# Attention stage of a decoder trunk: items joined over heads and groups, another order of branches, more work in the background

## The chip, the cores and the metric

The kernel runs on one core of a Trainium2 chip. The metric is the time of one execution on the device in microseconds (us). A core has five engines that run their own instruction streams and wait for one another through semaphores: TensorE (PE, with the weight loads PEld listed apart), VectorE (DVE), ScalarE (ACT), GpSimd (POOL) and SyncE (SP). Matrix products land in PSUM, in banks of 128 x 512 float32; everything else lies in SBUF. Transfers go over queues; in this kernel SP's queue carries the weights and ACT's a few others.

## The reference

A trunk of two layers on x of 512 tokens x 1024 channels. Layer 0 is a short convolution mixer and a squared-ReLU MLP. Then one shared key and value projection is made, layer 1 is sparse attention on it and a second MLP, and a final norm ends it. What matters here is the attention:

```python
kv = (h @ w_kv).reshape(B, S, 6, N_KV_GROUPS, HEAD_DIM)      # 6 parts of 4 groups x 64
k_cmp = compress_blocks(kv[:, :, 0], cmp_pe_k, phi_k_w1, phi_k_w2)   # 31 blocks of 32 tokens, stride 16
v_cmp = compress_blocks(kv[:, :, 1], cmp_pe_v, phi_v_w1, phi_v_w2)   # silu(flat @ w1) @ w2
k_sel, v_sel, k_win, v_win = kv[:, :, 2], kv[:, :, 3], kv[:, :, 4], kv[:, :, 5]
qg = h @ w_qg                          # 16 heads x 64, and 3 gates per head
q, gates = qg[..., :1024] / 8, sigmoid(qg[..., 1024:])
# for each block of 128 queries, each of 4 groups, each of 4 heads in the group:
o_c = softmax(q @ k_cmp.T + bias) @ v_cmp       # compressed branch
o_s = softmax(q @ ks.T + bias) @ vs             # selected blocks
o_w = softmax(q @ kw.T + bias) @ vw             # sliding window
o = gate0 * o_c + gate1 * o_s + gate2 * o_w
x = x + o @ w_o
```

With 512 tokens the selection (16 blocks of 64) and the window (512) hold all earlier tokens, so the second and third branch are both full causal attention, each with its own keys and values. The bias depends on the distance of the tokens and the head.

## The kernel before

**Arithmetic.** Every float32 operand is split into a high and a low float16 part, and a product is three matmuls into one accumulator (`mm3`, lines 339 to 341): high x high, low x high, high x low. Splits are made by ACT (high part) and DVE or POOL (low part).

**Weights.** They are cut into pieces of up to 512 KB in one list, `pieces`, in order of use. SP's queue loads them into `wst`; `convert_piece` makes `whi` on ACT (line 193) and `wlo` on DVE (line 194). `next_piece` hands out the next one, and `ahead_fine` converts up to two pieces ahead in steps between the matmuls.

**The stage that changes** lies between the last matmul of the first MLP and the first of the second. Each step of a projection is a generator that issues a few matmuls and yields:

- `keys(br)`, `values(br)`: keys and values of the second (br 0) and third (br 1) branch, into `KD` and `VT`; `gates()`; `queries(g)`: the four heads of group g into `Q`, whose low parts POOL makes (line 739).
- `raw(which)`: the raw keys or values of the compressed branch. 48 matmuls of 512 columns into two banks; then for each of the two banks DVE scales it into `at_s` (line 757), ACT and DVE split it into `kr_hl` (lines 360, 362), and six transfers on SP's queue (lines 763 to 765) lay it out in `big`. `kr_hl` has one buffer.
- `phi(which)`: the compressing MLP, 96 matmuls of 155 columns that read `big`, a Silu on ACT (line 793), a split, and a second small product.
- `out_proj(g)`: output projection of groups g and g + 1.

`load_T(g)` loads the bias rows of a group (issued on ACT's queue, line 621) and copies every sixteenth column to `Tc` on DVE (line 625).

A lead-in runs `keys(0)`, `keys(1)`, `values(0)`, `values(1)`, `gates` and `queries(0)` to their ends. Then come 144 **items**. A `Full` item is one head, one block `qb` of 128 queries and one branch: `nk` = 128 (qb + 1) keys. It goes through five steps:

- st0: scores on PE (lines 914, 915, bank b), bias and minimum on DVE (line 919), exponential with sum on ACT (line 922);
- st1: float32 transposes on PE (line 928, bank c), high part `at_ph` on ACT (line 931);
- st2: low part `at_pl` on DVE (line 934);
- st3: the product with the values on PE (lines 946 to 948, bank d); after the last head, gates and sums on DVE and POOL;
- st4: after a block's last part, its transposition into `ot`, which `out_proj` reads.

A `Cmp` item is the same for the compressed branch, for four heads of one group at once.

**Order.** The loop over items issues st0 of item i, then some background, then the later steps of earlier items (`lead`: 2, 3, 4 and 6 items back). A scheduler makes each engine's final order from the issued program; every engine then runs its own list in that order. The background is a chain of generators, resumed by a credit per item:

```python
items = full(0) + full(1) + cmps(0) + cmps(1) + full(2) + cmps(2) + cmps(3) + full(3)
# background: raw(0), q1, phi(0), raw(1), phi(1), q2, q3, then out_proj(0)
credit += 1.7 if i < 64 else 0.9          # yields per item
```

An item that needs something not yet made (its queries, the compressed keys and values) drains the background until it is there.

Of the kernel before, what the change touches and what calls it, by code (L numbers as in the profile page):

```python
# [10 lines left out]
F32 = mybir.dt.float32  # L11
# [37 lines left out]
def body(ctx, tc, x, rel_bias, norm_mix, norm_mlp, mlp_w1, mlp_w2, a_w_in, a_conv_w, a_w_out,  # L49
# [64 lines left out]
    for part in (2, 4, 3, 5):  # L114
        block(w_kv, part * 256)
    cols(b_w_qg[0], 1024, 48, SW)
    block(b_w_qg[0], 0)
    block(w_kv, 0)
    block(b_w_qg[0], 256)
# [5 lines left out]
    block(b_w_qg[0], 512)  # L125
# [472 lines left out]
    with pool("attn") as ap:  # L598
# [20 lines left out]
        def load_T(g):  # L619
            t = ap.tile([128, 4, TW], F32, name="T", bufs=2)  # L620
            nc.scalar.dma_start(t, bass.AP(tensor=ext_d.tensor, offset=ext_d.offset + 4 * g * EXT,
                                           ap=[[1, 128], [EXT, 4], [1, TW]]))
            TG[g] = t
            c = ap.tile([128, 4, 32], F32, name="Tc", bufs=4)
            DVE.tensor_copy(c, t[:, :, 0:512:16])
            TC[g] = c
# [19 lines left out]
        lead_in = [True]  # L646

# [3 lines left out]
        def gated_pair(xs, mid=None):  # L651

            po = [abank(), abank()]
            for half in range(2):
                w = next_piece()
                cv = ahead_fine()
                for c in range(4):
                    if mid and (half, c) == (1, 1):
                        mid()
                    for m in range(2):  # L660
# [4 lines left out]
                        yield  # L665
# [23 lines left out]
        def values(br):  # L689
# [4 lines left out]
            for t in range(4):  # L694
                for c in range(8):
# [6 lines left out]
                    yield  # L702
# [27 lines left out]
        def queries(g):  # L730
            po = yield from gated_pair(xq)
            q = ap.tile([128, 4, S], F16, name="Q", bufs=3)
# [13 lines left out]
        def raw(which):  # L746
# [7 lines left out]
            for m in range(2):  # L754
# [4 lines left out]
                hl = ap.tile([128, 2, S], F16, name="kr_hl", bufs=1)  # L759
# [11 lines left out]
        def phi(which):  # L771
            kr = KRs[which]
            ph = [bank("a"), bank("a")]
            for quarter in range(4):
                w = next_piece()
                cv = ahead_fine()
                for c in range(4):
# [7 lines left out]
                    yield  # L785
                drain(cv)
            hs = ap.tile([128, 2, 2, G, 32], F16, name="phi_h", bufs=1)
            DVE.memset(hs[:, :, :, :, 31:32], 0.0)
            for m in range(2):
                bcol = ap.tile([128, 1], F32, name="phi_b", bufs=2)  # L790
                ACT.activation(bcol, ph[m][:, 124:125], AF.Copy, scale=1.0 / (SW * SK))
# [7 lines left out]
            if which == 0:  # L799
                pk = bank("e")  # L800
# [9 lines left out]
            else:  # L810
                pv = bank("e")
                hd = ap.tile([128, 2, 2, G, 4, 32], F16, name="phi_hd")
# [10 lines left out]
                for g in range(4):  # L823
                    t = ap.tile([128, 4, 64], F32, name="vc_t", bufs=1)
# [11 lines left out]
        def out_proj(g):  # L836
            for p in range(4):
# [3 lines left out]
                for c in range(4):  # L841
                    for m in range(2):
# [3 lines left out]
                        yield  # L846
# [19 lines left out]
        og = {}  # L866
        parts = {}

        def add_part(g, qb, t):

            k = (g, qb)
            if g not in og:
                og[g] = ap.tile([128, 4, 256], F32, name="o", bufs=2)
            if k not in parts:
                parts[k] = 1
                return og[g][:, qb], False
            return og[g][:, qb], True

        def finish(g, qb):
# [5 lines left out]
            for i in range(2):  # L885
                PE.transpose(p[:, i * 128:(i + 1) * 128], og[g][:, qb, i * 128:(i + 1) * 128], ident)
            d = [u[:, 2 * g:2 * g + 2, qb * 128:(qb + 1) * 128] for u in ot]
            split_to(d[0], d[1], p[:, 0:256].rearrange("p (i q) -> p i q", i=2))
            if qb == 3:
                done.add(f"o{g}")  # L890

        class Item:
            def need(self):
                return []

        obank = {}

        class Full(Item):
            def __init__(self, g, qb, br, h):
                self.g, self.qb, self.br, self.h = g, qb, br, h  # L900
                self.nb = qb + 1
                self.nk = 128 * self.nb

            def need(self):
                return [f"q{self.g}"]

            def st0(self):
                g, qb, br, h, nk = self.g, self.qb, self.br, self.h, self.nk
                if (g, qb) not in obank:
                    obank[g, qb] = [None, ap.tile([128, 8], F32, name="l", bufs=3)]  # L910
                l = obank[g, qb][1]
                s = bank("b")
                q = Qs[g][:, h, qb * 128:(qb + 1) * 128]
                PE.matmul(s[:, :nk], q, KD[:, br, 0, g, :nk], start=True, stop=False)
                PE.matmul(s[:, :nk], q, KD[:, br, 1, g, :nk], start=False, stop=True)
                lg = ftile("at_s", 3)
                mn = ap.tile([128, 1], F32, name="at_m", bufs=3)
                lo = 128 * qb + PAD
                DVE.tensor_tensor_reduce(lg[:, :nk], s[:, :nk], TG[g][:, h, lo:lo - nk:-1], -1.0 / SL, 3e38,  # L919
                                         OP.add, OP.min, mn)  # L920
                self.p = ftile("at_p", 3)
                ACT.activation(self.p[:, :nk], lg[:, :nk], AF.Exp, bias=mn, scale=-1.0,  # L922
                               accum_out=l[:, br * 4 + h:br * 4 + h + 1])

            def st1(self):
                pt = bank("c")
                for b in range(self.nb):
                    PE.transpose(pt[:, b * 128:(b + 1) * 128], self.p[:, b * 128:(b + 1) * 128], ident)
                self.pt = [ap.tile([128, S], F16, name=n, bufs=3) for n in ("at_ph", "at_pl")]
                self.ps = pt[:, :self.nk]  # L930
                ACT.activation(self.pt[0][:, :self.nk], self.ps, AF.Copy, scale=SP)

            def st2(self):
# [305 lines left out]
```

## Time and profile before

| | |
|---|---|
| median of 3 runs | 1151.32 us (1150.67 to 1155.41) |
| the profiled execution | 1151.28 us, of which its span is 1149.5 us |
| PE busy | 1106.0 us, 96% of the span, 7959 matmuls |
| DVE busy | 837.8 us (73%) |
| ACT busy | 582.7 us (51%) |
| POOL busy | 162.2 us (14%) |
| the attention stage | 500.3 to 811.7 us, 311.4 us |

The span runs from the first instruction to the last. A time in front of a timeline row is us from the start of the span, the number behind it is the instruction's duration; a bracket at the end is the idle time of the engine before it and what ended it. A group of instructions shows their count, then total busy us and mean ns of one, then the idle time before them. L914 is line 914 of the kernel as printed above.

### The profile page before, as it was taken

The numbers are of one execution on the slowest core, as the hardware profiler recorded it, in microseconds if no ns is written. First come the engines' busy times: TensorE is split into PE (matmuls) and PEld (weight loads), VectorE is DVE, ScalarE is ACT, GpSimd is POOL, SyncE is SP. The second block draws the span as 40 slices with busy tenths as digits, with TensorE's granted clock in tenths as the row PEclk, the third lists the DMA queues.
The fourth block names the chain that finished last, engine by engine and source line by source line (L and its number), as shares of the span: only waits on it lengthen the run. The fifth ranks groups of instructions, "written<-read, shape, count | busy, mean of one in ns | idle before, by whom it ended". The sixth has DMA issues, their size and how long they took to land.

```text
span 1149.5 us, 20386 instructions
## 1 busy us (share of the span) xinstructions
PE 1106.0 (96%) x7959; PEld 694.1 (60%) x7959; DVE 837.8 (73%) x1604; ACT 582.7 (51%) x983; POOL 162.2 (14%) x211
## 2 busy tenths in 40 slices
PE   9999999999999999999999899999999999999996
PEld 4444444447884458868466665765444688445885
DVE  4755557765897557988487898997985588754795
ACT  4523235345333444457679778676644534343452
POOL 0000000422000220000120023111132200022031
PEclk9999999999999999999999999999999999999998
DMA  6433235433433333314333530111643343330231
GB/s 208 130 92 110 92 111 174 119 93 93 127 98 108 109 110 107 97 55 122 110 79 99 143 94 19 57 38 38 186 126 99 88 126 110 104 99 19 75 92 74
DMA packets 149379, 115.76 MB, mean 101 GB/s; under 512 B 8612, under 2 KB 146564, under 8 KB 149284
## 3 DMA queue, kind: packets, MB, share of 16 engines
q1 hardware_dynamic: 146736, 109.47, 31.8%
q10 hardware_dynamic: 2260, 4.40, 1.3%
q8 instruction: 62, 1.02, 0.4%
q0 software_dynamic: 288, 0.61, 0.2%
q14 instruction: 33, 0.27, 0.1%
HBM read 110.22 MB, written 2.14 MB: 98 GB/s over the span
## 4 chain that ended last, share of the span: by engine, by line
PE 49%; DVE 20%; ACT 12%; issue 8%; POOL 6%; DMA 4%; SPq 0%; DVEq 0%; ACTq 0%; POOLq 0%
POOL ml_z L501 6%; PE a L340 4%; PE a L339 4%; PE a L341 4%; DVE wlo L183 4%; DMA wst<-mlp_w_dram 4%; ACT rh L502 3%; PE b L339 3%; PE b L340 3%; PE b L341 3%; PE c L341 3%; PE c L339 3%; PE c L340 3%; DVE wst L180 3%; DVE wlo L194 3%
## 5 line engine op out<-in xcount | busy, mean ns | idle before, releaser
L193 ACT ACTIVATE whi<-wst 128x1024 f16<-128x1024 f32 (+2 forms) x171 | 142.2, 857 | 128.3 <-PE b L340 40.0
L194 DVE SCALAR_TENSOR_TENSOR wlo<-wst,whi 128x1024 f16<-128x1024 f32 (+2 forms) x171 | 168.1, 990 | 47.3 <-ACT whi L193 47.1
L501 POOL TENSOR_TENSOR ml_z<-ml_z 128x256 f32<-128x256 f32 x128 | 101.1, 811 | 604.5 <-ACT ml_z L499 403.9
L182 ACT ACTIVATE whi<-wst 128x1792 f16<-128x1792 f32 x64 | 107.0, 1692 | 132.6 <-DVE wst L180 107.8
L341 PEld LDWEIGHTS <-wlo 128*128 128x128 f16 x1024 | 100.1, 98 | 109.3 <-DVE wlo L194 0.7
L339 PEld LDWEIGHTS <-whi 128*128 128x128 f16 x1024 | 100.4, 98 | 108.1 <-issue 3.7
L503 DVE TENSOR_TENSOR rl<-ml_z,rh 128x1792 f16<-128x1792 f32 x32 | 64.8, 2025 | 136.9 <-ACT rh L502 136.9
L340 PEld LDWEIGHTS <-whi 128*128 128x128 f16 x1024 | 100.2, 98 | 105.0 <-issue 1.7
L183 DVE SCALAR_TENSOR_TENSOR wlo<-wst,whi 128x1792 f16<-128x1792 f32 x64 | 129.8, 2033 | 3.6 <-ACT whi L182 3.6
L180 DVE TENSOR_TENSOR wst<-wst 128x256 f32<-128x256 f32 x256 | 105.9, 455 | 24.1 <-DMA wst<-mlp_w_dram 23.1
L502 ACT ACTIVATE rh<-ml_z 128x1792 f16<-128x1792 f32 x32 | 54.3, 1697 | 103.4 <-POOL ml_z L501 103.4
L550 PEld LDWEIGHTS <-wlo 128*128 128x128 f16 x896 | 88.1, 98 | 16.6 <-issue 5.1
L549 PEld LDWEIGHTS <-whi 128*128 128x128 f16 x896 | 88.1, 98 | 14.8 <-issue 3.9
L548 PEld LDWEIGHTS <-whi 128*128 128x128 f16 x896 | 88.2, 98 | 11.0
L499 ACT ACTIVATE ml_z<-ml_t 128x1024 f32<-128x1024 f32 x32 | 33.8, 1057 | 90.5 <-DVE ml_t L497 90.5
L341 PE MATMUL b<-xsh,wlo 128*128 128x512 f16 x208 | 78.8, 379 | 0.0
L340 PE MATMUL b<-xsl,whi 128*128 128x512 f16 x208 | 78.8, 379 | 0.0
L339 PE MATMUL b<-xsh,whi 128*128 128x512 f16 x208 | 78.7, 379 | 0.0
L922 ACT ACTIVATE at_p<-at_s,at_m 128x128 f32<-128x128 f32 (+3 forms) x128 | 71.3, 557 | 13.4 <-DVE at_m L919 13.0
L549 PE MATMUL a<-rl,whi 128*128 128x256 f16 x256 | 70.3, 275 | 4.6 <-DVE rl L503 4.6
L339 PE MATMUL c<-xsh,whi 128*128 128x512 f16 x192 | 72.8, 379 | 0.0
L340 PE MATMUL c<-xsl,whi 128*128 128x512 f16 x192 | 72.8, 379 | 0.0
(312 smaller groups left out, 2757.5 us busy)
## 6 DMA issues: line engine op xcount, KB each, us to landing
wst<-mlp_w_dram SPq DMA_DIRECT2D x256, 256.0 KB, 3.4
wst<-a_w_in_dram SPq DMA_DIRECT2D x18, 512.0 KB, 3.6
wst<-w_kv_dram SPq DMA_DIRECT2D x12, 512.0 KB, 3.7
T<-ext_d ACTq DMA_DIRECT2D x4, 1056.0 KB, 6.0
wst<-a_w_out_dram SPq DMA_DIRECT2D x8, 512.0 KB, 3.5
wst<-b_w_qg_dram SPq DMA_DIRECT2D x8, 512.0 KB, 4.3
wst<-b_w_o_dram SPq DMA_DIRECT2D x8, 512.0 KB, 3.5
wst<-a_w_in_dram SPq DMA_DIRECT2D x8, 384.0 KB, 5.5
```

Of the source, the lines that this page charges most:

```text
L180: DVE.tensor_tensor(b[:, :, o], b[:, :, x], b[:, :, y], op=e)
L182: ACT.activation(hi, b[:, :, 1:], AF.Copy, scale=sc)
L183: DVE.scalar_tensor_tensor(lo, b[:, :, 1:], sc, hi, op0=OP.mult, op1=OP.subtract)
L193: ACT.activation(hi[:, s:e], w, AF.Copy, scale=sc)
L194: DVE.scalar_tensor_tensor(lo[:, s:e], w, sc, hi[:, s:e], op0=OP.mult, op1=OP.subtract)
L339: PE.matmul(ps, w[0], xs[0], start=start, stop=False)
L340: PE.matmul(ps, w[0], xs[1], start=False, stop=False)
L341: PE.matmul(ps, w[1], xs[0], start=False, stop=stop)
L501: POOL.tensor_tensor(z[:, o], z[:, a], z[:, b], op=e)
L502: ACT.activation(rh[0][:, p], z[:, 1:8], AF.Copy)
L548: PE.matmul(acc7[i], wh, xh, start=c == 0 and not other, stop=False, skip_group_check=other)
L549: PE.matmul(acc7[i], wh, xl, start=False, stop=False, skip_group_check=other)
```

## The change

- The order of the weight pieces follows a new order of work: the lead-in is `keys(0)`, `queries(0)`, `gates`. `values(0)`, q1, `keys(1)`, `values(1)`, q2, `raw(0)`, `phi(0)`, `raw(1)`, `phi(1)`, q3 and `out_proj(0)` are background.
- A yield now returns a number that stands for its work, and the credit is 1.25 per item until q3 is made, 0.9 behind it.
- A `Full` item takes four heads in query block 0, two in block 1 and one in blocks 2 and 3: 88 `Full` items. A `Cmp` item takes two groups (eight heads): 8 items.
- Order of the items: second branch of group 0, second of group 1, third of group 0, third of group 1 (44 items); then group 2 with the compressed items of groups 0 and 1, which start behind 10 items; then group 3, blocks 3 to 0, with those of groups 2 and 3.
- The products with the values take banks d and e in turn; compressed products and the second product of `phi` take bank c.
- Silu is computed as (tanh(v/2) + 1) v/2: a tanh and an add on ACT and a product on DVE.
- `Q` has four buffers; `kr_hl` is widened and shares its buffer with `phi_hd`; `load_T(1)` is called ahead of the items, the other two at items 37 and 45; partial outputs are added in `add_parts`.

```diff
-        for k in (marked("ks", keys(0)), marked("kw", keys(1)), values(0), values(1), gates(),
-                  marked("q0", queries(0))):
+        for k in (keys(0), marked("q0", queries(0)), gates()):
             drain(k)
...
-                hl = ap.tile([128, 2, S], F16, name="kr_hl", bufs=1)
+                hl = ap.tile([128, 4, S], F16, name="kr_hl", bufs=1)[:, 0:2]
...
-                ACT.activation(t, ph[m][:, 0:124].rearrange("p (g j) -> p g j", g=4), AF.Silu,
-                               bias=bcol, scale=1.0 / (SW * SK))
-                split_to(hs[:, m, 0, :, 0:31], hs[:, m, 1, :, 0:31], t, SR)
+                v = ph[m][:, 0:124].rearrange("p (g j) -> p g j", g=4)
+                ACT.activation(t, v, AF.Tanh, bias=bias[:, 1:2], scale=0.5 / (SW * SK))
+                ACT.activation(t, t, AF.Identity, bias=ones)
+                DVE.scalar_tensor_tensor(t, v, bias[:, 0:1], t, op0=OP.add, op1=OP.mult)
+                split_to(hs[:, m, 0, :, 0:31], hs[:, m, 1, :, 0:31], t, 0.5 * SR / (SW * SK))
...
             def need(self):
-                return [f"q{self.g}"]
+                return [f"q{self.g}"] + (["k1"] if self.br else [])
+
+            def need3(self):
+                return [f"v{self.br}"]
...
-                PE.matmul(s[:, :nk], q, KD[:, br, 0, g, :nk], start=True, stop=False)
-                PE.matmul(s[:, :nk], q, KD[:, br, 1, g, :nk], start=False, stop=True)
+                for j, h in enumerate(self.heads):
+                    q = Qs[g][:, h, qb * 128:(qb + 1) * 128]
+                    o = s[:, j * nk:(j + 1) * nk]
+                    PE.matmul(o, q, KD[:, br, 0, g, :nk], start=True, stop=False)
+                    PE.matmul(o, q, KD[:, br, 1, g, :nk], start=False, stop=True)
...
+                for j, h in enumerate(self.heads):
+                    w = slice(j * nk, (j + 1) * nk)
+                    DVE.tensor_tensor_reduce(lg[:, w], s[:, w], TG[g][:, h, lo:lo - nk:-1], -1.0 / SL, 3e38,
+                                             OP.add, OP.min, mn[:, j:j + 1])
+                    ACT.activation(self.p[:, w], lg[:, w], AF.Exp, bias=mn[:, j:j + 1], scale=-1.0,
+                                   accum_out=l[:, br * 4 + h:br * 4 + h + 1])
...
+                ACT.activation(self.pt[0], self.ps, AF.Copy, scale=SP)
...
-        items = full(0) + full(1) + cmps(0) + cmps(1) + full(2) + cmps(2) + cmps(3) + full(3)
+        def heads_of(qb):
+            n = max(1, 4 >> qb) if qb < 2 else 1
+            return [tuple(range(h, h + n)) for h in range(0, 4, n)]
...
+        A = branch(0, 0) + branch(1, 0) + branch(0, 1) + branch(1, 1)
+        B = mixed(both(2, (0, 1, 2, 3)), [Cmp(0, qb) for qb in range(4)], 10, 3)
+        C = mixed(both(3, (3, 2, 1, 0)), [Cmp(1, qb) for qb in (3, 2, 1, 0)], 4, 4)
+        items = A + B + C
+        at_item = {len(A) - 7: lambda: load_T(2), len(A) + 1: lambda: load_T(3)}
+        load_T(1)

         def background():
+            yield from marked("v0", values(0))
+            yield from marked("q1", queries(1))
+            yield from marked("k1", keys(1))
+            yield from marked("v1", values(1))
+            yield from marked("q2", queries(2))
             yield from raw(0)
-            yield from marked("q1", queries(1))
             yield from phi(0)
             yield from raw(1)
             yield from marked("cmp", phi(1))
-            yield from marked("q2", queries(2))
             yield from marked("q3", queries(3))
             while "o1" not in done:
                 yield "wait"
             yield from out_proj(0)
...
-            credit += 1.7 if i < 64 else 0.9
-            while credit >= 1.0:
-                run_bg(1)
-                credit -= 1.0
+            credit += 1.25 if "q3" not in done else 0.9
+            while credit > 0.0:
+                u = next(bg, "end")
+                if u in ("wait", "end"):
+                    credit = 0.0
+                else:
+                    credit -= u or 0.1
```

Every need of an item (`ensure`) still drains the background until what is needed is there: an item of the compressed branch until `phi(1)` is done.

More of the change, by code (lines that the diff above doesn't have):

```diff
@@ L1007, in st1 @@
+                self.pt = [ap.tile([128, S], F16, name=n, bufs=3)[:, :self.w] for n in ("at_ph", "at_pl")]
+                self.ps = pt[:, :self.w]
                 ACT.activation(self.pt[0], self.ps, AF.Copy, scale=SP)
@@ new lines, in heads_of, with branch, both, mixed @@
+        def heads_of(qb):
+            n = max(1, 4 >> qb) if qb < 2 else 1
+            return [tuple(range(h, h + n)) for h in range(0, 4, n)]
+        def branch(g, br):
+            return [Full(g, qb, br, hs) for qb in range(4) for hs in heads_of(qb)]
+        def both(g, order):
+            return [Full(g, qb, br, hs) for qb in order for br in range(2) for hs in heads_of(qb)]
+        def mixed(items, extra, start, step):
+            r = []
+            for i, it in enumerate(items):
+                k, m = divmod(i - start, step)
+                if i >= start and m == 0 and k < len(extra):
+                    r.append(extra[k])
+                r.append(it)
+            assert len(r) == len(items) + len(extra)
+            return r
@@ L1059, in body, with ensure @@
         bg = background()
-        def run_bg(n):
-            for _ in range(n):
-                if next(bg, "end") in ("wait", "end"):
-                    return
+        def ensure(names):
+            for k in names:
+                while k not in done:
+                    if next(bg, "end") in ("wait", "end"):
+                        raise RuntimeError(k)
         lead = {1: 2, 2: 3, 3: 4, 4: 6}
```

334 lines of the change are left out of this document (171 added, 163 removed).

## The prediction

> **The bound now.** I read the page first, then the busy time by stage, the waits, and the timeline where the change cuts.
>
> ```profile
> span 1149.5 us, 20386 instructions
> PE 1106.0 (96%) x7959; PEld 694.1 (60%) x7959; DVE 837.8 (73%) x1604; ACT 582.7 (51%) x983; POOL 162.2 (14%) x211
> PEclk9999999999999999999999999999999999999998
> ```
>
> TensorE is busy in 96% of the span, at full clock nearly throughout. So time comes from its gaps, or from fewer matmuls. The change touches one stretch only, from the first key projection to the first matmul of the second MLP. In the windows view this stretch is the first row; three parts of it follow (columns: window, its length, then busy time of PE, PEld, DVE, ACT and POOL, PE clock, DMA share, GB/s):
>
> ```profile
> 500.30:811.70 311.40, 291.93 (x2861) 192.52 (x2860) 258.12 (x776) 229.50 (x607) 45.46 (x62) 1.00 0.28 81
> 556.70:660.00 103.30, 92.54 (x954) 62.58 (x953) 78.52 (x244) 82.62 (x225) 14.35 (x14) 1.00 0.36 100
> 660.00:710.00 50.00, 48.22 (x507) 31.71 (x507) 46.95 (x173) 38.90 (x120) 13.38 (x21) 1.00 0.21 65
> 710.00:786.00 76.00, 71.50 (x781) 49.03 (x780) 71.54 (x245) 56.91 (x169) 14.82 (x20) 1.00 0.14 43
> ```
>
> Busy time flatters PE, because a matmul's drain counts as busy. What the work needs at least is read from start-to-start spacings on the timeline, where nothing waits:
>
> ```profile
> 500.31 0.38 PE L339 MATMUL a<-xsh,whi 128*128 128x512 f16 x1
> ...
> 506.57 0.38 PE L341 MATMUL a<-xsh,wlo 128*128 128x512 f16 x1
> 667.38 0.60 PE L928 MATMUL c<-ident,at_p 128*128 128x128 f32 x4
> 667.81 0.19 PE L946 MATMUL d<-VT,at_ph 128*128 128x64 f16 x1
> ...
> 668.16 0.38 PE L914 MATMUL b<-KD,Q 128*128 128x512 f16 x1
> 649.34 0.23 PE L339 MATMUL a<-big,whi 128*128 128x155 f16 x1 [0.70 <-issue]
> 649.41 0.23 PE L340 MATMUL a<-big,whi 128*128 128x155 f16 x1
> ```
>
> The first two rows are 29 matmuls apart: 6.26/29 = 0.216 us for 512 columns. Four f32 transposes take 667.81 - 667.38 = 0.43, so 0.108 each; twelve 64-column matmuls take 0.35, so 0.029 each; 155 columns take 0.07. 256 and 384 columns I take in proportion to 512 (0.109, 0.163). The stretch holds 640 of 512 columns (138.2), 372 f32 transposes (40.4), 304 of 256 (33.1), 64 of 384 (10.4), 192 of 155 (13.4), 984 of 64 (28.5) and 298 smaller ones (about 10): 274 to 275 us, say 274.8. So 311.4 - 274.8 = 36.6 us are lost before. The same sum by window gives 18.1 of the 103.3, 5.8 of the 50.0, 9.4 of the 76.0, 2.9 in the last 25.7 and 0.4 in the lead-in.
>
> What loses them is a chain of short steps over three engines, as the waits view shows (who, for whom: total us, count, mean):
>
> ```profile
> ACT at_ph L931 <- PE c L928: 16.8, 30, 1.2
> ```
>
> ACT waits for PE's transposes, not the reverse alone: scores, bias, exponential, transposes, split and V product follow one another, and PE needs other matmuls to fill the time. Those come from the background generators.
>
> **The base of the sum.** In the built order of the changed kernel the stretch issues the same 2,854 matmuls, shape by shape. Joining takes no matmul out. So: time after = time before - 36.6 + what is lost after. The profiled execution took 1151.3 us (span 1149.5, 1.8 around it), which is the median of the runs (1151.32), so one base serves for both.
>
> **Joined items.** The bias and minimum and the exponential stay one instruction per head; only the split pair (lines 931, 934) is shared, by 4 heads in query block 0 and by 2 in block 1.
>
> ```profile
> L934 DVE SCALAR_TENSOR_TENSOR at_pl<-c,at_ph 128x128 f16<-128x128 f32 x32 | 8.9, 284 | 1.8 <-ACT at_ph L931 1.7
> L934 DVE SCALAR_TENSOR_TENSOR at_pl<-c,at_ph 128x512 f16<-128x512 f32 x32 | 21.8, 685 | 1.8 <-ACT at_ph L931 1.5
> L922 ACT ACTIVATION_READ_ACCUMULATOR at_p<-at_s,at_m 128x1 f32 x128 | 24.6, 192 | 0.0
> L922 ACT ACT_TABLE_LOAD x4 | 5.1, 1283 | 0.1
> ```
>
> Four blocks of 128 cost 4 x 0.284 = 1.14 us of DVE, one of 512 costs 0.685: at most 0.45 saved per group and branch in block 0, about 0.15 per pair in block 1. Over 8 groups and branches that is at most 6 us of DVE's 258, and about as much of ACT's 230. The 128 accumulator reads (24.6 us) stay. None of this is on PE; it counts only where DVE or ACT limits, and is contained in the loads below.
>
> **Tanh for Silu.** The order keeps two table loads in the stretch where eight stood: six fewer, 6 x 1.283 = 7.7 us of ACT, beside PE mostly; two small ACT and two DVE instructions come in. The trace has 0.1 us idle before the four loads together, and the next ACT instruction starts right behind. The Trainium skill ("ScalarE: Activation LUTs", section "What ACT_TABLE_LOAD costs") adds a drain of about 1.38 us to each switch, which would make it 16 us; the row shows no such idle time, so the trace does not bear that out here. I take no PE time for it by itself: it loosens the chain, and is in the loss rates.
>
> **Start** (3 to 8 us, take 5). Lead-in shrinks to keys(0), q0 and gates; values, second keys and q1 go behind the items.
>
> ```profile
> 504.90 0.41 ACTq L621 DMA_DIRECT2D T<-ext_d  x1
> 506.38 4.38 ACT L288 ACTIVATE xqh<-X,vec 128x512 f16<-128x512 f32 x7
> T<-ext_d ACTq DMA_DIRECT2D x4, 1056.0 KB, 6.0
> L739 POOL TENSOR_TENSOR Q<-at_s,Q 64x512 f16<-64x512 f32 x16 | 19.2, 1197 | 72.7 <-ACT Q L738 71.8
> ```
>
> In the new order T(0)'s transfer is issued behind the xqh splits, so at 510.8, and lands 6.0 later, at 516.8. DVE's copy Tc waits for it, and queued behind that copy is the last step of the row scales rs_r, for which PE's broadcast waits: about 1 us of PE. Then POOL makes q0's low parts, 4 x 1.2 = 4.8 us, with only the gates' 96 matmuls of 48 columns on PE beside them (at most 96 x 0.029 = 2.8 us), and the first item now wants all four heads before values(0) may follow on PE: 2.4 to 4. Twice the wait at T gives the upper end.
>
> **First part** (items with projections: 4 to 12 us, take 6.5). From the gates to the end of raw0 there are 107 us of matmuls, 81 us of DVE and 76 of ACT by the same kinds of spacing. Before, 85 us of such work took 103.3 with DVE and ACT at 78.5 and 82.6: a loss of 18. After, the loads are a quarter below PE's, items are longer and background spread evenly. The lower end is 4%, the upper the 12% of the two later windows (5.8 of 50, 9.4 of 76); I stand at 6%, nearer the lower, because here neither DVE nor ACT fills the time as DVE does there.
>
> **Compressed branch.** This is the step that costs. The first compressed item is number 54 of 96, and everything that it needs is drained ahead of it: the rest of raw0, phi0, raw1, phi1 stand in PE's order almost without items between. Between raw and phi lies a chain off PE. The timeline of before, where items covered it:
>
> ```profile
> 631.13 0.38 PE L341 MATMUL a<-xsh,wlo 128*128 128x512 f16 x1
> 632.42 1.01 DVE L757 TENSOR_TENSOR at_s<-a,rb 128x512 f32<-128x512 f32 x1
> 633.47 0.63 ACT L360 ACTIVATE kr_hl<-at_s 128x512 f16<-128x512 f32 x1 [0.27 <-DVE at_s L757]
> 634.88 0.68 DVE L362 TENSOR_TENSOR kr_hl<-at_s,kr_hl 128x512 f16<-128x512 f32 x1
> 635.62 0.60 SPq L763 DMA_DIRECT2D big<-kr_hl  x1
> 638.88 0.61 SPq L765 DMA_DIRECT2D big<-kr_hl  x1
> 641.83 0.62 ACT L360 ACTIVATE kr_hl<-at_s 128x512 f16<-128x512 f32 x1
> 642.48 0.69 DVE L362 TENSOR_TENSOR kr_hl<-at_s,kr_hl 128x512 f16<-128x512 f32 x1
> 647.37 0.61 SPq L765 DMA_DIRECT2D big<-kr_hl  x1
> ```
>
> Scaling, split, six transfers issued in turn; then, as kr_hl has one buffer, the second half waits until the first six have landed (641.83), splits, issues six more; phi's first matmul is at 649.34. That is 18.2 us from the last raw matmul. Without items on DVE the first issue comes 2.9 us behind the matmul and not 4.5: about 15 to 17 us remain.
>
> From raw0 to phi0 the order has 9.7 us of item matmuls there, with 14.5 of DVE. Loss 15 to 17 less 9.7, and more where items starve: 4 to 9, take 7.
>
> From raw1 to phi1 the order has only 1.25 us of matmuls there (16 small scores, 18 V products, two scores of 384). Loss 11 to 16, take 13. The low end needs the first half's transfers to land faster than traced.
>
> Then there are the seams, phi0 to raw1 and phi1 to q3, where bank a is emptied with no items beside it: 1 to 4 each; the nearest rows are the 1.01 us of scaling at 632.42 and the 0.63 us of ACT behind it. Take 2.5 each, 5 together.
>
> **The clock** behind these gaps (0 to 7 us, take 3). The trace shows once what idle time does to it:
>
> ```profile
> 913.00:922.00 9.00, 6.43 (x32) 4.52 (x32) 6.10 (x4) 5.75 (x5) 0.00 (x0) 0.62 0.24 71
> 913.78 0.27 PE L548 MATMUL a<-rh,whi 128*128 128x256 f16 x1 [1.05 <-ACT rh L502]
> 915.84 0.37 PE L549 MATMUL a<-rl,whi 128*128 128x256 f16 x1 [1.79 <-DVE rl L503]
> 916.01 0.42 PE L550 MATMUL a<-rh,wlo 128*128 128x256 f16 x1
> 916.22 0.42 PE L548 MATMUL a<-rh,whi 128*128 128x256 f16 x1
> ```
>
> Idles of 1.05 and 1.79 us, and then 0.21 us per matmul of 256 columns instead of 0.109. The window's clock of 0.62 means (1 - 0.62) x 9 = 3.4 us of full speed missing, up to 6.8 at half. One such slow spell behind the 13 us gap, none behind the smaller: 3; two: 7. The Trainium skill ("TensorE: Matmul & The Clock Gate", Part 1) has the rule that an idle window drops the array to half rate and a busy one restores it; the row agrees, and by its smaller cost, some 1.7 us a restart, the term would be about 2.
>
> **Remaining items** (up to the projection 3 to 9 us, take 5.5; behind it 3 to 8, take 5). From phi1 to the first output projection the order has 34.6 us of matmuls and 35 of DVE; before, 44.2 of matmuls with 47 of DVE took 50.0, a loss of 5.8. Behind it 50.8 of matmuls with 36 to 38 of DVE, then the last projection, 19 with little beside it: before, the last 25.7 lost 2.9; 4% of 50.8 is added as 2.
>
> **Sum.** 5 + 6.5 + 7 + 13 + 5 + 3 + 5.5 + 5 = 50.0, between 30 and 77 by the ends. 1151.3 - 36.6 + 50.0 = 1164.7, say 1165.
>
> **Rivals.**
>
> Faster. Long items and evenly spread background leave the attention parts at 2 to 4% loss, and the compressed gap is half hidden since transfers land faster on an idle queue. At losses of 30 us, every term at its low end, the time is 1144.7; it decides below 31 us. For it: 11 us or so less to lose in the first part, and six table loads gone. Against it: 11 us in one gap that nothing in the order covers. 0.12.
>
> About equal: gaps at the low ends, items as taken, no slow clock: 5 + 6.5 + 5 + 11 + 3 + 0 + 4 + 4 = 38.5, so 1153. 0.20.
>
> Heavier: slow clock twice (7), the first part at 12%: 50 + 4 + 5.5 = 59.5 and the items behind phi1, bound by DVE, at 9 make 63: 1178; beyond 1181 if transfers wait for weight loads on SP's queue as well. 0.13.
>
> The change doesn't do what it says: joining leaves ACT and DVE nearly as loaded, as worked out above. That is in the forecast and moves it by at most the first part's spread.
>
> **How the numbers follow.** Forecast (1157 to 1173) 0.55, heavier 0.13, equal 0.20, faster 0.12. A measurement tells 0.5% here, 5.8 us: faster is below 1145.5, slower above 1157. That gives faster 0.12, same 0.20, slower 0.68. The range leaves out the far side of faster and heavier: 1148 to 1181.
>
> **What would show it.** The new trace should have one idle stretch of PE of 11 us or more between raw1's last 512-column matmul and phi1's first of 155, a smaller one ahead of phi0, and possibly 0.2 us spacings behind. rs_r should come after Tc, near 517. DVE should be the busiest beside PE behind phi1. I am wrong if the gap is under 6 us, if the first part loses over 15, or if the stretch is shorter than 306 us.

## The result and the profile after

The changed kernel takes 1170.94 us (median of 4 runs, 1169.18 to 1173.19), against 1153.37 for the kernel before (4 runs): a ratio of 1.0152, 95% interval 1.0115 to 1.0190. It is slower, by 17.6 us where 14 were forecast. The profiled executions differ by 1167.4 - 1149.5 = 17.9 us of span.

The page of the changed kernel, the lines that answer to those of before:

```profile
span 1167.4 us, 20139 instructions
PE 1103.2 (95%) x7959; PEld 697.5 (60%) x7959; DVE 835.2 (72%) x1527; ACT 571.4 (49%) x924; POOL 159.1 (14%) x201
```

PE, DVE, ACT and POOL each have a little less to do (DVE 2.6 us, ACT 11.3 us), and the span is longer: this is waiting, not work. The windows view of the changed kernel, first the whole stage, then its parts in order (columns as in the prediction):

```profile
498.70:830.50 331.80, 291.92 (x2861) 197.39 (x2860) 257.24 (x702) 218.21 (x548) 44.50 (x52) 0.97 0.26 77
523.90:533.10 9.20, 6.24 (x58) 4.68 (x56) 6.48 (x18) 8.30 (x18) 4.95 (x4) 1.00 0.18 59
533.10:642.35 109.25, 103.73 (x1015) 71.74 (x1013) 83.81 (x248) 79.37 (x207) 14.24 (x14) 1.00 0.21 65
642.35:660.41 18.06, 13.07 (x169) 10.02 (x168) 16.62 (x60) 14.31 (x47) 1.46 (x2) 0.91 0.56 148
683.96:698.49 14.53, 1.41 (x37) 1.19 (x36) 4.02 (x6) 2.39 (x4) 0.00 (x0) 0.69 0.46 108
698.49:707.32 8.83, 8.83 (x96) 8.79 (x96) 2.04 (x4) 2.52 (x5) 0.00 (x0) 0.74 0.22 64
709.30:727.30 18.00, 17.93 (x163) 10.88 (x163) 16.35 (x51) 11.40 (x32) 1.47 (x2) 1.00 0.27 88
727.30:755.92 28.62, 22.09 (x260) 16.14 (x260) 24.82 (x58) 20.23 (x46) 9.62 (x9) 0.94 0.06 20
755.92:830.48 74.56, 72.17 (x657) 45.50 (x657) 64.15 (x176) 47.39 (x121) 11.06 (x18) 1.00 0.18 55
```

The stage takes 331.8 us with the same 2,861 matmuls (311.4 before); the rest of the program is 2.5 us shorter. With the prediction's spacings (work 274.8 us), the ledger of lost time is:

| part of the stage | forecast | measured |
|---|---|---|
| lead-in, start and first part, up to the end of raw0 | 11.5 | 12.0 |
| raw0 to phi0 | 7 | 8.4 |
| seams, with raw1's own items | 5 | 4.3 |
| raw1 to phi1 | 13 | 13.3 |
| phi1 at less than full clock | 3 | 2.2 |
| items from q3 up to the output projection | 5.5 | 12.1 |
| behind it | 5 | 4.7 |
| sum | 50.0 | 57.0 |

The large gap, on the timeline of the changed kernel:

```profile
683.74 0.38 PE L343 MATMUL a<-xsh,wlo 128*128 128x512 f16 x1
684.57 0.63 ACT L362 ACTIVATE kr_hl<-at_s 128x512 f16<-128x512 f32 x1
686.76 0.60 SPq L771 DMA_DIRECT2D big<-kr_hl  x1
690.02 0.60 SPq L773 DMA_DIRECT2D big<-kr_hl  x1
691.96 0.63 ACT L362 ACTIVATE kr_hl<-at_s 128x512 f16<-128x512 f32 x1 [6.24 <-DMA big<-kr_hl]
693.34 0.60 SPq L771 DMA_DIRECT2D big<-kr_hl  x1
696.59 0.61 SPq L773 DMA_DIRECT2D big<-kr_hl  x1
698.49 0.29 PE L341 MATMUL a<-big,whi 128*128 128x155 f16 x1 [13.12 <-DMA big<-kr_hl]
698.58 0.33 PE L342 MATMUL a<-big,whi 128*128 128x155 f16 x1
698.71 0.33 PE L343 MATMUL a<-big,wlo 128*128 128x155 f16 x1
```

It is the chain of the prediction, step for step: split, six transfers, landing (ACT is idle for 6.24 us until then), split, six more, phi. PE stands for 13.12 us, and then phi1 runs with 0.13 us between matmuls of 155 columns where 0.07 is full clock.

### The profile page after: what moved, and what is told of

Read it like the earlier page. It is cut to its first block, busy times and chain, and to the rows that moved or that the text cites. A ratio compares the mean times of both kernels' runs of the same rounds, so it can differ in the third digit from the quotient of the medians.

```text
span 1167.4 us, 20139 instructions
## 1 busy us (share of the span) xinstructions
PE 1103.2 (95%) x7959; PEld 697.5 (60%) x7959; DVE 835.2 (72%) x1527; ACT 571.4 (49%) x924; POOL 159.1 (14%) x201
## 4 chain that ended last, share of the span: by engine, by line
PE 41%; DVE 22%; ACT 13%; issue 9%; POOL 8%; DMA 5%; SPq 1%; DVEq 0%; ACTq 0%; POOLq 0%
POOL ml_z L503 7%; DVE wlo L185 5%; PE a L341 5%; PE a L342 5%; PE a L343 5%; DMA wst<-mlp_w_dram 4%; ACT rh L504 4%; DVE wlo L196 3%; DVE wst L182 3%; DVE ml_t L499 3%; PE b L342 2%; PE b L341 2%; ACT ml_z L501 2%; PE b L343 2%; PE c L341 2%
## 5 line engine op out<-in xcount | busy, mean ns | idle before, releaser
L195 ACT ACTIVATE whi<-wst 128x1024 f16<-128x1024 f32 (+3 forms) x170 | 142.0, 860 | 142.6 <-PE a L342 48.8
L196 DVE SCALAR_TENSOR_TENSOR wlo<-wst,whi 128x1024 f16<-128x1024 f32 (+3 forms) x170 | 167.4, 992 | 54.6 <-ACT whi L195 54.4
L551 PEld LDWEIGHTS <-whi 128*128 128x128 f16 x896 | 87.6, 98 | 14.5 <-issue 4.0
L964 ACT ACTIVATE at_p<-at_s,at_m 128x128 f32<-128x128 f32 (+3 forms) x128 | 70.9, 555 | 35.0 <-DVE at_m L962 34.6
L341 PE MATMUL a<-xsh,whi 128*128 128x512 f16 x192 | 72.8, 379 | 1.9 <-DVE phi_t L806 1.9
L343 PE MATMUL c<-xsh,wlo 128*128 128x512 f16 x192 | 72.8, 379 | 0.0
L343 PE MATMUL b<-xsh,wlo 128*128 128x512 f16 x192 | 72.8, 379 | 0.0
```

The lines of the kernel that those rows point to most:

```text
L195: ACT.activation(hi[:, s:e], w, AF.Copy, scale=sc)
L196: DVE.scalar_tensor_tensor(lo[:, s:e], w, sc, hi[:, s:e], op0=OP.mult, op1=OP.subtract)
L341: PE.matmul(ps, w[0], xs[0], start=start, stop=False)
L343: PE.matmul(ps, w[1], xs[0], start=False, stop=stop)
L551: PE.matmul(acc7[i], wh, xl, start=False, stop=False, skip_group_check=other)
```

## The experiments

Each kernel is compared with runs of the kernel before on the same chip. "Lost" is by the same ledger on the profiled run: the length of a stretch less what its matmuls need at the prediction's spacings.

**Two halves of kr_hl.**

```diff
+            hls = ap.tile([128, 4, S], F16, name="kr_hl", bufs=1)
             for m in range(2):
...
-                hl = ap.tile([128, 4, S], F16, name="kr_hl", bufs=1)[:, 0:2]
+                hl = hls[:, 2 * m:2 * m + 2]
```

> The changed kernel, with the two halves of a raw projection split into the two halves of one kr_hl tile, so that the second half's split does not wait until the first six transfers have landed. Theory A (the time went into the uncovered chain between raw and phi): the second six transfers are issued right behind the first six, the chain shortens by some 3.7 us (landing 2.3 and split 1.4), the idle stretch ahead of phi1 goes from 13.3 to 9 to 10 us, the one ahead of phi0 loses 2 to 3 us: 6 us less in all, about 1165. Rival B (the time went into the new order of items and its waits, and whatever a gap gives is given back behind it): within 2 us of the changed kernel's 1171.

Measured: 1169.16 us, ratio 1.0137 (1.0108 to 1.0167), not told apart from the changed kernel's 1.0152; it lies where rival B was put, not theory A. The mechanism is there, its size is not:

```profile
690.87 0.60 SPq L774 DMA_DIRECT2D big<-kr_hl  x1
691.58 0.59 SPq L772 DMA_DIRECT2D big<-kr_hl  x1
694.82 0.61 SPq L774 DMA_DIRECT2D big<-kr_hl  x1
```

The second six transfers (from 691.58) follow the first six at once, where the changed kernel waited 2.7 us between. But now twelve issues of 0.65 us in turn are the chain: from the end of raw1 to phi1 it takes 12.0 us instead of 14.5, and loses 10.8 instead of 13.3. The stage is 3.2 us shorter (328.6), the time 1.8.

**Queries of group 3 in the gap.**

```diff
             yield from raw(1)
+            yield from marked("q3", queries(3))
             yield from marked("cmp", phi(1))
-            yield from marked("q3", queries(3))
```

> The changed kernel, with the queries of group 3 projected between raw(1) and phi(1) instead of behind phi(1); the weight pieces follow. Same work. Theory A: 10.4 us of matmuls stand in the gap, its idle time goes from 13.3 to 3 to 4 us, the half clock of phi1 (2.2 us) goes, and the items behind phi1, which lose q3 as their cover, give back 3 to 4: 7 to 9 us less, about 1163. Rival B: all of it is given back, about 1171.

Measured: 1166.79 us, ratio 1.0119 (1.0090 to 1.0149). The gap loses 4.0 instead of 13.3, phi1 runs at full clock, the stage is 6.9 us shorter (324.9). What is given back stands behind phi1, in the windows view of this kernel:

```profile
707.10:748.95 41.85, 33.46 (x375) 23.57 (x374) 37.28 (x106) 29.20 (x76) 6.20 (x7) 0.88 0.12 39
```

24.2 us of item matmuls with no projection beside them take 41.9 us: 17.7 lost where the changed kernel lost 14.0 in a longer stretch, DVE busy for 37.3. Nearly 4 us more went in unchanged code: what follows the stage took 340.7 us, against 336.9 in the changed kernel's profile. So theory A holds for the gap, and rival B in part for the items: the time is 4.1 us shorter, between the two expectations.

**More background per item.**

```diff
-            credit += 1.25 if "q3" not in done else 0.9
+            credit += 1.6 if "q3" not in done else 0.9
```

> The changed kernel with 1.6 us of background per item instead of 1.25 until q3 is made, so that the compressed branch is not drained all at once ahead of the first compressed item: in the order 7.2 us of item matmuls stand between raw1 and phi1 where 1.25 stood. Theory A: the idle stretch there goes from 13.3 to 7 or 8 us, 5 to 6 us less, about 1165. Rival B: the items behind have that much less cover, 1169 to 1172.

Measured: 1181.73 us, ratio 1.0253 (1.0221 to 1.0285): both expectations missed. (The profiled execution is the longest of the four, 1185.54 us.) The two gaps in the windows view of this kernel, raw0 to phi0 and raw1 to phi1, and from its waits view over the stage what DVE waited for (total us, count, longest; the last number of the prediction's waits row is the longest too, not the mean):

```profile
639.30:662.30 23.00, 12.30 (x127) 8.35 (x125) 14.58 (x44) 8.76 (x21) 2.19 (x3) 0.78 0.53 139
688.40:708.00 19.60, 8.91 (x138) 6.90 (x137) 12.14 (x30) 9.39 (x25) 2.56 (x3) 0.88 0.34 81
DVE Tc L628 <- DMA T<-ext_d: 7.6, 2, 4.7
```

The items stand in the second gap as planned (7.1 us of matmuls), and it grew from 14.5 to 19.6 us. The items stand on DVE and ACT ahead of the chain's splits: the first transfer is issued 6.5 us after the last raw matmul (688.2 to 694.7), where it took 3.0 us in the changed kernel (683.7 to 686.8). Besides, DVE now stands at the Tc copies for 7.6 us in all until their transfers have landed (0.9 in the changed kernel), 4.7 of them in the first gap.

**Silu back, and tanh alone on the kernel before.**

```diff
...
-                ACT.activation(t, v, AF.Tanh, bias=bias[:, 1:2], scale=0.5 / (SW * SK))
-                ACT.activation(t, t, AF.Identity, bias=ones)
-                DVE.scalar_tensor_tensor(t, v, bias[:, 0:1], t, op0=OP.add, op1=OP.mult)
...
+                ACT.activation(t, ph[m][:, 0:124].rearrange("p (g j) -> p g j", g=4), AF.Silu,
+                               bias=bcol, scale=1.0 / (SW * SK))
...
```

> The changed kernel with the Silu of before in phi in place of tanh, identity and product. Table loads come back (two or more per phi, 1.28 us each on ACT). If they stand beside idle or busy PE they cost nothing: 1171 within 2 us. If the load stands on the chain behind phi, where ACT splits for the next step, 1.3 us per phi, 1173 to 1174. If the tanh path was the slower one (two more instructions on the chain of each half), 1169 to 1170.

> The kernel before with only the tanh form in phi. If the table loads stand on the chain there as they do in the changed kernel (where putting Silu back cost 5 us): about 1148. If they are hidden there behind items: 1152 to 1154.

Silu back, measured: 1175.96 us, ratio 1.0190 (1.0155 to 1.0225). That interval overlaps the changed kernel's, though the runs themselves don't (1173.59 to 1176.31 against 1169.18 to 1173.19); no expectation was met. Around phi its ledger is the changed kernel's (8.3, 13.3, 1.9 lost); 3 us more are lost ahead of raw0 and 3 behind the stage, where nothing was changed. So the five microseconds are not shown to be the four table loads that came back. The other way round, the kernel before with tanh alone, and six table loads fewer in the stage, took 1153.88 us, ratio 1.0004 (0.9990 to 1.0018): there the loads cost nothing that can be measured. (The Trainium skill, "ScalarE: Activation LUTs", section "What ACT_TABLE_LOAD costs", puts about 2.66 us on each switch of tables; no run here shows a price on the path.)

**The old order with the other parts of the change.** Lead-in, pieces, background and items in the order of before:

```diff
-        items = A + B + C
+        items = (both(0, qbs) + both(1, qbs) + [Cmp(0, qb) for qb in qbs] + both(2, qbs)
+                 + [Cmp(1, qb) for qb in qbs] + both(3, qbs))
```

> The changed kernel with the lead-in, the piece order, the background order and the item order of before put back; joined items, compressed items over two groups, tanh, banks and credit 1.25 stay. Theory A (order, short lead-in and drained background cost the time): the gap between raw1 and phi1 has 7 us of item matmuls again and the one ahead of phi0 is spread: 1148 to 1155. Rival C (the joined items or the changed banks themselves are slower): 1165 or more.

Measured: 1168.81 us, ratio 1.0120 (1.0102 to 1.0138). This falls on rival C's side. The stage takes 328.7 us and loses 53.9, with other places: 8.2 between phi0 and the end of raw1, 12.3 from raw1 to phi1 under 7.0 us of items, and TensorE's clock is lower there. The two windows, and the wait at the end of phi0 on the timelines of DVE and PE:

```profile
614.90:643.40 28.50, 24.22 (x216) 15.59 (x214) 20.07 (x80) 19.22 (x65) 1.46 (x2) 0.88 0.29 89
643.40:662.80 19.40, 10.68 (x114) 7.91 (x113) 12.16 (x31) 8.87 (x24) 1.11 (x1) 0.75 0.35 82
622.74 0.27 DVE L626 COPY Tc<-T 128x128 f32<-128x128 f32 x1 [2.06 <-DMA T<-ext_d]
623.32 0.61 PE L339 MATMUL a<-xsh,whi 128*128 128x512 f16 x1 [2.08 <-DVE phi_t L804]
```

So the order of before is not enough for the time of before: putting it back gave 2 to 4 us of the 17.6 (by the medians or by the ratios). Something of what stayed (compressed items of eight heads, banks, credit, the times of the T loads) costs in it. One share shows in the two rows: the Tc copy stands in DVE's order ahead of phi0's product, and DVE and then PE stand for 2.1 us until its transfer has landed; the clock is at 0.50 from 622.25 to 629.07. The others these runs don't tell apart; that it is not the joining, the next two kernels show, and tanh alone cost nothing on the kernel before.

**One head per item.**

```diff
-            n = max(1, 4 >> qb) if qb < 2 else 1
+            n = 1
...
-        B = mixed(both(2, (0, 1, 2, 3)), [Cmp(0, qb) for qb in range(4)], 10, 3)
+        B = mixed(both(2, (0, 1, 2, 3)), [Cmp(0, qb) for qb in range(4)], 20, 3)
...
-            credit += 1.25 if "q3" not in done else 0.9
+            credit += 0.82 if "q3" not in done else 0.9
```

> The changed kernel with one head per full item again (128 full items, credit 0.82 per item, first compressed item at the same place). The prediction's term (joining saves a few us of DVE and ACT beside PE): 1170 to 1175. Rival C (joining lengthens the chain and costs): 1160 to 1166. Rival D (joining is what keeps the loss down, because items are longer): over 1178.

Measured: 1180.83 us, ratio 1.0226 (1.0211 to 1.0242): rival D. Without joining, and with the credit set anew for the greater number of items, the changed kernel is 10 us slower. It loses 14.5 from raw0 to phi0 instead of 8.4, and 8.0 behind the start of the output projection instead of 4.7.

**Joining alone, on the kernel before.** Full items of 4, 2, 1 and 1 heads; background per head as it was:

```diff
-            return [Full(g, qb, br, h) for qb in range(4) for br in range(2) for h in range(4)]
+            n = (4, 2, 1, 1)
+            return [Full(g, qb, br, tuple(range(h, h + n[qb]))) for qb in range(4) for br in range(2)
+                    for h in range(0, 4, n[qb])]
...
-            credit += 1.7 if i < 64 else 0.9
+            n = len(items[i].heads) if i < len(items) and isinstance(items[i], Full) else 1
+            credit += n * (1.7 if i < 44 else 0.9)
```

> The kernel before with one part of the change alone: full items of four heads in query block 0 and two in block 1; order, lead-in, background and its credit per head stay as before. In the changed kernel, one head per item cost 10 us more, all of it where items had no background beside them. If joining does that by taking work off DVE and ACT, it helps here too, less, since fewer items stand without cover: 1146 to 1150. The prediction's reading (a few us of DVE and ACT beside PE): 1151 to 1154. If a joined item's longer chain costs where items have cover: 1156 or more.

Measured: 1145.66 us (6 runs), ratio 0.9944, interval 0.9922 to 0.9966. This version is faster than both kernels, by some 0.6% and 2%. Its stage and the part from the output projection on, in the windows view:

```profile
499.00:806.40 307.40, 290.06 (x2860) 194.18 (x2859) 253.85 (x736) 224.66 (x566) 46.29 (x62) 0.99 0.28 82
707.20:806.40 99.20, 95.16 (x980) 62.74 (x980) 89.56 (x269) 71.75 (x189) 17.54 (x24) 1.00 0.15 44
```

The stage takes 307.4 us for 311.4 before and loses 32.6; the part from the projection on loses 8.6 where 12.5 were lost. The medians differ by 7.6 us, the profiled executions by 6.2; 4.0 of these are in the stage, the rest stands in code that is the same.

**Filling the gap.**

```diff
+            junk = bank("c")
+            for _ in range(48):
+                PE.matmul(junk, xkv[0][:, 0, 0:128], xkv[0][:, 0], start=True, stop=True)
             yield from marked("cmp", phi(1))
```

> The changed kernel with 48 matmuls of 512 columns more, between raw(1) and phi(1), into a bank that nothing reads: 10.4 us of PE in a stretch where it waits. If the slow phi1 (8.8 us instead of 6.7) comes from the idle time ahead, it runs at full clock here, 2 us less: 1169. If the idle time has nothing to do with it, phi1 stays at 8.8 and the time at 1171.

Measured: 1169.66 us (two runs), 1.3 below the changed kernel's median, within what runs differ. The filler ran 10.5 us at full clock, then PE still waited for the last transfers, and phi1 was slow again. This kernel's row at phi1, phi1's window and two windows of 3.41 us around its start, and then the same of the kernel with group 3's queries in the gap:

```profile
700.88 0.23 PE L341 MATMUL a<-big,whi 128*128 128x155 f16 x1 [2.75 <-DMA big<-kr_hl]
700.90:709.20 8.30, 8.30 (x96) 8.21 (x96) 2.09 (x4) 2.57 (x5) 0.00 (x0) 0.79 0.22 68
698.11:701.52 3.41, 0.66 (x11) 0.67 (x11) 0.00 (x0) 0.00 (x0) 0.00 (x0) 1.00 0.42 89
701.52:704.93 3.41, 3.41 (x30) 3.41 (x28) 0.29 (x1) 0.31 (x1) 0.00 (x0) 0.50 0.02 5
700.39 0.23 PE L341 MATMUL a<-big,whi 128*128 128x155 f16 x1 [3.25 <-DMA big<-kr_hl]
700.40:707.10 6.70, 6.70 (x96) 6.62 (x96) 2.25 (x5) 2.57 (x5) 2.29 (x2) 1.00 0.51 159
695.04:698.45 3.41, 2.10 (x29) 1.25 (x27) 1.94 (x3) 2.37 (x4) 1.12 (x1) 1.00 0.75 196
698.45:701.86 3.41, 1.47 (x22) 1.50 (x23) 0.69 (x1) 1.29 (x3) 3.19 (x4) 1.00 0.23 51
```

2.75 us of idle time were followed by a clock of 0.79, and 3.25 us by full clock. The length of one idle stretch alone doesn't decide; where it falls does. In the traces of all fourteen kernels the clock between 500 and 840 us is 1.00 or 0.50, and it changes only on a grid of 3.41 us (in the changed kernel at 648.52, 651.93, 689.48, 703.13, 740.68 and 744.09). The windows of 3.41 us above are slots of that grid. The filler kernel's idle time falls into one slot, in which PE is busy for 0.66 us, and the next slot runs at 0.50; in the other kernel it is spread over two, with 2.10 and 1.47 us of PE, and the clock stays at 1.00. In these traces every slot at full clock with less than 1.4 us of PE was followed by a slow one, and none with more than 1.9 us; in between both occur.

**Two queues for the transfers**, on the kernel before and on the changed one with everything that shortens or covers the chain:

```diff
+                    qu = nc.sync if s == 0 else nc.scalar
-                    nc.sync.dma_start(kr[0:64, :, g, :], hl[r])
+                    qu.dma_start(kr[0:64, :, g, :], hl[r])
...
```

> The kernel before, with the raw projection's two halves split into the two halves of one kr_hl tile (it shares its buffer with phi_hd, as in the changed kernel) and half of its transfers issued on ACT's queue. Its chain from raw1 to phi1 took 18.0 us and lost 8.4 there under 9.6 us of items. With no wait for landing (2.3 and a split of 1.4) and six issues of 0.65 in turn instead of twelve, the chain takes 10 to 11: 4 to 6 us less, 1148 to 1150. Rival: as the items in the gap wait for one another on DVE and ACT, what is not lost there is lost by the same items later: 1152 to 1155.

> The changed kernel with queries of group 3 in the gap, the two halves of one kr_hl tile and half of the transfers on ACT's queue: everything that shortens or covers the chain. Theory A: the gap ahead of phi1 (4.0 us lost with queries of group 3 in it) goes to under 1, the one ahead of phi0 (8.2) to 3 or 4: 1158 to 1161, still behind the kernel before, because the items behind phi1 lose 17 us without cover. Rival B: 1166 to 1168.

Measured: 1156.72 us on the kernel before, ratio 1.0030 (1.0018 to 1.0043): 3.4 us slower, and above both expectations. From raw1 to phi1 it takes 12.2 us instead of 18.0 and still loses 7.4 (8.4 before), because only 4.9 us of items stand there instead of 9.6; they come later, and the stretch up to the projection loses 9.6 instead of 6.2. What the rival said of the items is seen, though it did not foresee a loss. On the changed kernel: 1164.97 us, ratio 1.0104 (1.0091 to 1.0117), not the 1158 to 1161 expected of theory A, and just under rival B's 1166 to 1168. The gap ahead of phi1 is gone (0.7 lost), but the items without cover lose 11.6 from raw0 to phi0 and 18.7 behind phi1.

**A spare buffer for o_t.**

```diff
-            t = ap.tile([128, 512], F32, name="o_t", bufs=1)[:, 0:nb * nh * 64].rearrange(
+            t = ftile("at_s", 4)[:, 0:nb * nh * 64].rearrange(
```

(The other users of at_s share that ring of four.)

> The changed kernel with the partial outputs o_t in a ring of four with at_s instead of one buffer of their own, so that DVE's product does not wait until POOL has added the one before (POOL's adds stand behind 5.2 us of the low parts of group 3's queries). If that wait is what made the stretch from phi1 to the output projection lose 14.0 us: 9 to 11 there, and 1166 to 1168. If DVE's own load and the lack of background limit there: 13 to 14, and 1170 to 1172.

Measured: 1173.03 us, ratio 1.0172 (1.0159 to 1.0185). From phi1 to the projection 14.2 are lost for 14.0. The wait behind POOL is on the timeline of the changed kernel (the first three rows; the last is the same matmul in this kernel),

```profile
730.91 5.16 POOL L747 TENSOR_TENSOR Q<-at_s,Q 64x512 f16<-64x512 f32 x4 [2.22 <-ACT Q L746]
737.44 0.69 DVE L898 TENSOR_TENSOR o_t<-e,rl 128x512 f32<-128x512 f32 x1 [1.54 <-POOL o L903]
738.79 0.18 PE L1027 MATMUL b<-KC,Q 128*128 128x32 f16 x1 [1.99 <-DVE at_m L962]
741.65 0.19 PE L1027 MATMUL b<-KC,Q 128*128 128x32 f16 x1 [0.50 <-DVE at_m L962]
```

and taking it away shortened PE's wait from 1.99 to 0.50 us, but the time did not follow: what was gained was lost again behind it, where the clock stood at 0.50 for 6.83 us and not for 3.41.

## Why the prediction was right, and where not

**Direction** was right, and so was the place of the greatest loss. The forecast was 1165 in a range of 1148 to 1181, and 1170.94 came. The base held: equal matmuls (the trace holds four small ones more than the 2,854 counted, 0.1 us), and a changed kernel that differs by what PE waits. The step on the compressed branch was the best sized: 7 and 13 us forecast, 8.4 and 13.3 measured. That the gap is the cause of the loss that stands in it, group 3's queries show: put into it, they took 9.3 us off its loss.

**The main cause** is shown in part only. Covering the gap gave 4.1 us of time with group 3's queries in it, and 6.0 us with two queues as well, which left 0.7 us of its loss; putting the old order back gave 2 to 4. So more than half of the 17.6 us does not go with the gap or the order alone.

**Failed: the remaining items up to the projection.** Forecast 5.5, measured 12.1. I priced 34.6 us of matmuls as one stretch, at the loss of a traced window in which projections stand beside the items. The two rows 709.30 and 727.30 above show what was missed: as long as q3's matmuls last, 0.7 of 18.0 us is lost; without them 11.4 of 28.6, in which the clock was 0.94. The step should have been split where the background ends. Items alone take their time from the chain over DVE and ACT: 9.6 us of item matmuls in 18.0 (before, raw1 to phi1), 9.6 in 18.1 (changed, raw0 to phi0), 7.1 in 19.6 (more credit), 24.2 in 41.9 (q3 in the gap), 17.3 in 28.6 (changed, here). PE's matmuls need 36 to 60% of the time there; with projections beside them it was 107 us in 118.5 (rows 523.90 and 533.10). DVE is busy for 87 to 93% of these stretches, but for the one with more credit (62%), where the chain's transfers are waited for. The two such stretches of the kernel before, in its windows view:

```profile
631.34:649.34 18.00, 12.75 (x142) 8.22 (x141) 16.68 (x51) 13.96 (x43) 1.84 (x2) 1.00 0.58 156
702.10:709.79 7.69, 7.12 (x76) 4.82 (x76) 7.31 (x31) 7.69 (x30) 0.73 (x1) 1.00 0.24 71
```

The change has two such stretches and an empty gap, together 8.4 + 13.3 + 11.4 = 33.1 us lost, where the kernel before lost 8.4 in one such stretch and 2.6 in a short one ahead of its output projection. That is 22 us, and the stages differ by 20.4: this says where the loss stands, and not yet which part of the change brought it.

**Failed: joining as a matter of a few us of DVE and ACT beside PE.** It is worth 10 us in the changed order and 6 to 8 alone on the kernel before, 4.0 of them in the stage. The saving of work that I worked out is real (DVE is busy for 253.9 us of that stage, for 258.1 before), but I put it beside PE, where work on DVE and ACT costs nothing. The gain stands where DVE has little room: among items alone (raw0 to phi0, 6 us), and behind the start of the output projection, where most of the 4.0 us were gained on the kernel before. The prediction's own row 710.00 has DVE busy there for 71.5 of 76.0 us. That DVE's load is the reason fits these numbers; no run took it alone.

**Failed in its reason: the start.** T(0)'s transfer is not behind the splits; T(1)'s is:

```profile
503.32 0.40 ACTq L623 DMA_DIRECT2D T<-ext_d  x1
510.52 0.38 ACTq L623 DMA_DIRECT2D T<-ext_d  x1
512.57 0.27 DVE L628 COPY Tc<-T 128x128 f32<-128x128 f32 x1
512.76 0.15 DVE L305 SCALAR_TENSOR_TENSOR rs_r<-rs_t,rs_r 128x4 f32<-128x4 f32 x1
```

rs_r came at 512.8, not near 517, with no wait. What is lost at the start (3.6 us, row 523.90) is the other half of that step, POOL making the low parts of q0 for four heads: four times the weights of PE's first scores wait for POOL there (0.8 to 1.5 us each). The first part lost 7.9 behind it, where 6.5 were forecast. That the two together came out near (11.5 forecast, 12.0 measured with the lead-in) is luck: 3.6 came for 5, and 7.9 for 6.5.

**The clock** was sized about right at phi1 (2.2 for 3). It came twice more, unforeseen, for 3.41 us each: between raw0 and phi0, where the prediction had none (row 642.35, 0.91), and among the items behind q3 (row 727.30, 0.94).

**The rivals.** The faster one needed the gap half hidden; nothing hid it. The heavier one had the right place, the items behind phi1, but for the wrong amount (9 for 12.1). That joining does little was counted as a rival that moves the time by no more than the first part's spread: the runs show that it is the part of this change that brings something, and that the rest of the change takes away more. Which of the rest is open: with the old order put back it still does.

**Open:** which of the parts common to the changed kernel and to the one with the old order (eight-head compressed items, banks, credit, T loads) costs its share, apart from the 2.1 us at the Tc copy; and the 5 us of the Silu kernel.

## What to carry to other kernels

Price a stretch of a bound engine by what stands beside it, and split it where its filler ends: here a stretch of items took a tenth more time than its matmuls need with projections beside them, and two thirds to nine tenths more without (nearly three times as much where they shared DVE and ACT with a chain of transfers, in the kernel with more credit). Filler that is moved forward, or a chain that is shortened, is paid back in part where the items then stand bare. Of a bundle of changes, run each part on the old kernel: here one part alone gained 0.6% and the bundle lost 1.5%.

## What the runs showed that I had not expected

An idle stretch of 3.25 us ahead of phi1 was followed by full clock, one of 2.75 us by a clock of 0.79: what counted was how little PE did in one slot of 3.41 us. The unchanged part behind the stage took between 336.7 us and 340.7 us in the profiled runs of these kernels, so that a stage shorter by 6.9 us showed 4 us in the time. And the scheduled order changed with the chain: on the kernel before, the order made for the faster chain put 4.9 us of items into the gap, the one for the slower chain 9.6.
